# The loads of the heads' queries, keys and values in a memory cross-attention, chained in the order of their use

## Chip, core and metric

The kernel runs on one core of a Trainium2 chip. A core has a matmul engine (PE, with its weight loads shown apart as PEld), a vector engine (DVE), a scalar engine (ACT), a general engine (POOL) and a sync engine (SP), each with its own queue of instructions that it works off in order; a transfer (DMA) is issued from such a queue and then runs beside it. The metric is the device time of one execution in microseconds, lower is better, given as the median of three runs.

## The reference

One layer of an encoder is applied to two groups of tokens, 512 "sample" tokens (S) and 256 "prompt" tokens (P), with a width of 1024, in float32: a gated feed-forward block, a mixer, an attention over a memory of 256 tokens for each group, and a second feed-forward block, each followed by a layer norm. The change lies in the attention:

```
def memory_cross_attention(x, mem, w_q, w_kv, w_o):
    q = (x @ w_q).reshape(B, T, XA_HEADS, XA_HEAD_DIM)          # 4 heads of 256
    k, v = jnp.split(mem @ w_kv, 2, axis=-1)
    ...
    s = jnp.einsum('bthd,bmhd->bhtm', q, k) * (XA_HEAD_DIM ** -0.5)
    p = jax.nn.softmax(s, axis=-1)
    o = jnp.einsum('bhtm,bmhd->bthd', p, v).reshape(B, T, D_MODEL)
    return o @ w_o
```

## The kernel before

Every float32 matrix product is made of three matmuls on operands that are split into a high part and a rest (`split`, L84 on ACT and L85 on DVE; `mm3`, L103 to L105 on PE). A program orders the instructions of each engine ahead of the run; `tc.issue_after(x)` tells it that what is issued inside comes after x.

The attention (function `attention`) has these stages. Keys and values of both memories are made first (`keys_values`, run in pieces between other work, the rest of it by `drain()`, L1194). They don't stay on the chip: each head's keys go to a buffer in device memory (`kd[h]`), its values to `vd[h]`. Then the queries of the four heads are made, one head at a time, by `products` (L472) from sums of the input that lie in the tiles qS1, qS2 and qS4 (each as a high and a low tile, in the pool "sums"); each head's queries go to `qd[h]` by two stores (L1229, issued from ACT). The weights for a head's queries are loaded and combined by `weights_of` (loads L444).

Then the heads are worked off. `scores(h, s)` multiplies queries with keys (tile sc), takes the row maximum (DVE, L1259), the exponentials (ACT, L1264) and divides by the row sums (half on POOL, L1267, half on DVE, L1268). `probs_T(h, s)` transposes the result (tile pT, L1277) and splits it into tile p. `values(h, s)` multiplies it with the values (tile ov) and splits the result into xh and xl. The loop that orders them does, for h = 0, 1, 2: the scores of head h+1 for S, the transposes of head h for S, the scores of head h+1 for P, the transposes of head h for P, the value products of head h for both; the scores of head 0 stand ahead of it, the transposes and value products of head 3 run inside `tok_out`, the product with w_o (tile to). So a head's queries and keys are needed one pass before its values.

`fetch(h, parts)` brings a head's parts back: 12 KB per partition of queries (q), 8 KB of keys (k), 8 KB of values (v), each by one transfer issued from SP (L1213). Queries and keys of even heads go to the pool "even", those of odd heads to the pool "odd", one tile each, so that head 2's take the place of head 0's, and head 3's that of head 1's; values take turns in two tiles of "odd". The pool "odd" is opened once "sums" is closed and takes its memory, so that its first loads wait until PE has read the sums for the last time. SP issues in order: a load that waits holds all that is behind it in SP's queue, among it the weights of w_o (raw, L93), which are told to come after the last fetch (L1321).

Of the kernel before, what the change touches and what calls it, by code (L numbers as in the profile page):

```python
# [7 lines left out]
F32 = mybir.dt.float32  # L8
# [47 lines left out]
def _encoder(ctx, tc, nc, io, out, dbg):  # L56
# [6 lines left out]
    def psum(name):  # L63
        return pp.tile([128, 512], F32, tag="ps", name=name)
# [13 lines left out]
    def nid(p):  # L78
        uid[0] += 1
        return f"{p}{uid[0]}"  # L80
# [21 lines left out]
    def mm3(o, lh, ll, rh, rl, start, stop):  # L102
        nc.tensor.matmul(o, lh, rh, start=start, stop=False)  # L103
        nc.tensor.matmul(o, lh, rl, start=False, stop=False)  # L104
        nc.tensor.matmul(o, ll, rh, start=False, stop=stop)  # L105
# [89 lines left out]
    def fill(ns):  # L195
        while ns > 0 and pending:
            try:
                ns -= next(pending[0])
            except StopIteration:
                pending.pop(0)  # L200

    def drain():
        fill(1e12)
# [878 lines left out]
    def attention():  # L1082
# [9 lines left out]
        def opened(name, side="left"):  # L1092
            stack[name] = ExitStack()
            return stack[name].enter_context(tc.tile_pool(name=name, bufs=1, reuse_waits="tile", side=side))
# [75 lines left out]
        def ring(offs, n):  # L1170
            turn = [0]

            def get():
                turn[0] += 1
                o = offs[turn[0] % len(offs)]
                return flat[:, o:o + n]
            return get
# [4 lines left out]
        _, weights_of, _, products, _ = seven(X, sg, 1, ring([n * 512 for n in range(4)], 512), snap_t, sum_t)  # L1182
# [7 lines left out]
            last_sum = sums(X, (snap_t, sum_t), k, *a)  # L1190
        fill(FILL[2])
        wq = io["w_xq"]
        marks["dve"] = last_sum
        drain()  # L1194
        ws = weights_of(wq[0], wq[1])
        stack["mem"].close()

        ev, od = opened("even", "right"), None
        tl, last_fetch = {}, [None]

        def fetch(h, parts):
            pool = ev if h % 2 == 0 else od
            for p in parts:
                if p == "q":
                    t = pool.tile([128, 2, 2, TT], F32R, tag="q", bufs=1, name=nid("q"))
                    src = qd[h][:]
                elif p == "k":
                    t = pool.tile([128, 2, 2, 512], F32R, tag="k", bufs=1, name=nid("k"))
                    src = kd[h][:]
                else:  # L1210
                    t = od.tile([128, 4, 2, 256], F32R, tag="v", bufs=2, name=nid("v"))
                    src = vd[h][:]
                last_fetch[0] = nc.sync.dma_start(t[:].bitcast(F32), src)  # L1213
                tl[p, h] = t

        fetch(0, "k")
        qs = opened("qs", "right")
        for h in range(4):
            g1, x, u1, u2 = products(ws)
            for b, parts in ((1, (u1, u2)), (0, (g1, x))):  # L1220
                t = qs.tile([128, 2, TT], F32R, tag="qst", bufs=2, name=nid("qst"))
                for n, p in enumerate(parts):
                    hi, lo = [t[:, y, n * HT:(n + 1) * HT] for y in range(2)]
                    nc.scalar.activation(hi, p, AF.Copy, scale=-1.0 if b else 1.0)
                    if b:
                        ins = V.scalar_tensor_tensor(lo, p, -1.0, hi.bitcast(F32), ALU.mult, ALU.subtract)
                    else:
                        ins = V.tensor_tensor(lo, p, hi.bitcast(F32), op=ALU.subtract)
                nc.scalar.dma_start(qd[h][:, b], t[:].bitcast(F32))  # L1229
            marks["dve"] = ins.ins  # L1230
            if h < 3:
                with behind():
                    ws = weights_of(wq[2 * h + 2], wq[2 * h + 3])
            if h == 1:
                fetch(0, "q")
        stack["qs"].close()
        stack["sums"].close()
        od = opened("odd")
        fetch(1, "qk")
        fetch(0, "v")  # L1240

        es, pr = {}, {}

        def scores(h, s):
            q, kk = tl["q", h], tl["k", h]
            m0 = 0 if s is S else 256
            ms = slice(m0, m0 + 256)
            e2 = sg.tile([128, 1024], F32, tag="stg" if s is S else "raw", bufs=2 if s is S else 1, name=nid("e"))
            es[h, s] = e2
            for tp in range(s.nt // 2):  # L1250
                ps = psum(nid("sc"))
                for u in range(2):
                    tcs = slice(s.off + (2 * tp + u) * 128, s.off + (2 * tp + u + 1) * 128)
                    for b in range(2):
                        mm3(ps[:, u * 256:(u + 1) * 256], q[:, b, 0, tcs], q[:, b, 1, tcs],
                            kk[:, b, 0, ms], kk[:, b, 1, ms], b == 0, b == 1)
                mx = sp.tile([128, 2], F32, tag="mx", name=nid("mx"))
                sm = sp.tile([128, 2], F32, tag="sm", name=nid("sm"))
                V.tensor_reduce(mx[:], ps[:].rearrange("p (a b) -> p a b", b=256), AX.X, ALU.max)  # L1259
                V.tensor_scalar(mx[:], mx[:], -1.0 / 16, None, ALU.mult)  # L1260
                e = e2[:, tp * 512:tp * 512 + 512]
                for u in range(2):
                    us = slice(u * 256, (u + 1) * 256)
                    nc.scalar.activation(e[:, us], ps[:, us], AF.Exp, bias=mx[:, u:u + 1], scale=1.0 / 16,  # L1264
                                         accum_out=sm[:, u:u + 1])
                V.reciprocal(sm[:], sm[:])
                nc.gpsimd.tensor_scalar(e[:, 0:256], e[:, 0:256], sm[:, 0:1], None, ALU.mult)  # L1267
                V.tensor_scalar(e[:, 256:512], e[:, 256:512], sm[:, 1:2], None, ALU.mult)  # L1268

        def probs_T(h, s):  # L1270
            p = od.tile([128, 2, 2, s.T], F32R, tag="p" + s.name, bufs=1, name=nid("p"))
            pr[h, s] = p
            for m in range(2):
                ps = psum(nid("pT"))
                for t in range(s.nt):
                    c = t * 256 + m * 128
                    nc.tensor.transpose(ps[:, t * 128:(t + 1) * 128], es[h, s][:, c:c + 128], ident[:])  # L1277
                split(p[:, m, 0, :], p[:, m, 1, :], ps[:, :s.T])

        def values(h, s):  # L1280

            v, p = tl["v", h], pr[h, s]
            m0 = 0 if s is S else 2
            for b in range(2):
                ps = psum(nid("ov"))[:, :s.T]
                c = slice(b * 128, (b + 1) * 128)
                for m in range(2):
                    mm3(ps, v[:, m0 + m, 0, c], v[:, m0 + m, 1, c], p[:, m, 0, :], p[:, m, 1, :], m == 0, m == 1)
                split(xh[s.name][:, 2 * h + b, :], xl[s.name][:, 2 * h + b, :], ps)
# [3 lines left out]
        for h in range(3):  # L1293
            scores(h + 1, S)
            probs_T(h, S)
            scores(h + 1, P)
            if h < 2:
                fetch(h + 2, "qk")
            fetch(h + 1, "v")
            probs_T(h, P)  # L1300
            values(h, S)
            values(h, P)
# [128 lines left out]
    mixer(1)  # L1431
    x3 = dp.tile([128, 6, D], F32, name="x3")
    attention()
    ffn_fast(2, 3, front2, [0, 1, 2, 3, 4, 5], x3, ((9, 10), (1, 2), (3, 4), (5, 6)), [0, 7, 8])
    glob["accp"].close()
# [80 lines left out]
```

## Time and profile before

| | |
|---|---|
| median of 3 runs | 1778.63 us (1777.95 to 1780.29) |
| the profiled execution, its own time | 1777.02 us |
| its span in the profile | 1775.2 us |
| PE busy | 1748.7 us (99% of the span) |
| DVE / ACT / POOL busy | 1266.5 / 753.0 / 38.6 us |
| all DMA | 271.96 MB, 153 GB/s over the span |

The page gives the busy time of each engine over the span; the chain of waits follows the work that ended last back from its end; the timeline lists instructions in order with the idle time ahead of them and what ended it; the table of windows gives busy time, granted PE clock and DMA rate for chosen stretches. All times are microseconds from the start of the span. The scores, transposes and value products lie between 1150 and 1215 us.

### The profile page before, as it was taken

The numbers are of one execution on the slowest core, as the hardware profiler recorded it, in microseconds if no ns is written. First come the engines' busy times: TensorE is split into PE (matmuls) and PEld (weight loads), VectorE is DVE, ScalarE is ACT, GpSimd is POOL, SyncE is SP. The second block draws the span as 40 slices with busy tenths as digits, with TensorE's granted clock in tenths as the row PEclk, the third lists the DMA queues.
The fourth block names the chain that finished last, engine by engine and source line by source line (L and its number), as shares of the span: only waits on it lengthen the run. The fifth ranks groups of instructions, "written<-read, shape, count | busy, mean of one in ns | idle before, by whom it ended". The sixth has DMA issues, their size and how long they took to land.

```text
span 1775.2 us, 24813 instructions
## 1 busy us (share of the span) xinstructions
PE 1748.7 (99%) x9518; PEld 1605.4 (90%) x9518; DVE 1266.5 (71%) x2191; ACT 753.0 (42%) x1303; POOL 38.6 (2%) x72
## 2 busy tenths in 40 slices
PE   9999999999999999999999999979999999999998
PEld 9999999988899999888888888968899999998886
DVE  8777777597668654678775975555887777766966
ACT  6444444453235544645232243442244444444431
POOL 0000000000100000000000000020000000000002
PEclk9999999999999999999999999989999999999999
DMA  5433333687333334211464545475324333327951
GB/s 197 140 121 116 125 125 107 214 312 257 124 112 109 125 125 141 84 48 49 136 207 156 189 143 193 160 311 189 132 74 138 116 125 121 127 98 292 339 179 71
DMA packets 106038, 271.96 MB, mean 153 GB/s; under 512 B 10400, under 2 KB 32672, under 8 KB 104384
## 3 DMA queue, kind: packets, MB, share of 16 engines
q1 hardware_dynamic: 91776, 239.97, 38.9%
q10 hardware_dynamic: 14144, 30.41, 4.5%
q8 instruction: 74, 1.21, 0.3%
q14 instruction: 44, 0.36, 0.1%
HBM read 206.12 MB, written 64.23 MB: 152 GB/s over the span
## 4 chain that ended last, share of the span: by engine, by line
PE 95%; DVE 2%; DMA 2%; ACT 1%; issue 0%; SPq 0%; ACTq 0%; DVEq 0%
PE px L472 24%; PE dn L283 13%; PE py L472 12%; PE pz L472 6%; PE pt L103 5%; PE pt L104 5%; PE pt L105 5%; PE to L103 2%; PE to L105 2%; PE to L104 2%; PE dn L105 2%; PE dn L104 2%; PE dn L103 2%; PE pp L472 1%; PE lt L188 1%; PE V L105 1%
## 5 line engine op out<-in xcount | busy, mean ns | idle before, releaser
L84 ACT ACTIVATE wh<-raw 128x512 fp32r<-128x512 f32 (+2 forms) x281 | 221.0, 789 | 266.6 <-PE pt L104 83.8
L85 DVE TENSOR_TENSOR wl<-raw,wh 128x512 fp32r<-128x512 f32 (+2 forms) x281 | 248.7, 887 | 94.2 <-ACT wh L84 93.9
L283 PE MATMUL dn<-wh,ao 128*128 128x512 f32 x600 | 185.3, 389 | 0.0
L283 PEld LDWEIGHTS dn<-wh,ao 128*128 128x128 f32 x600 | 112.6, 188 | 23.5
L103 PE MATMUL pt<-xh,wh 128*128 128x512 f32 (+2 forms) x384 | 129.9, 338 | 0.0
L104 PE MATMUL pt<-xl,wh 128*128 128x512 f32 (+2 forms) x384 | 129.3, 337 | 0.0
L105 PE MATMUL pt<-xh,wl 128*128 128x512 f32 (+2 forms) x384 | 128.9, 336 | 0.0
L84 ACT ACTIVATE wh<-tt 128x512 fp32r<-128x512 f32 x156 | 94.0, 624 | 72.0 <-PE px L472 60.5
L283 PE MATMUL dn<-wl,ao 128*128 128x512 f32 x300 | 116.7, 389 | 0.0
L85 DVE TENSOR_TENSOR wl<-tt,wh 128x512 fp32r<-128x512 f32 x156 | 104.0, 685 | 3.0 <-ACT wh L84 2.2
L472 PE MATMUL px<-xh,wl 128*128 128x384 f32 x280 | 93.5, 334 | 0.0
L472 PE MATMUL px<-xh,wh 128*128 128x384 f32 x280 | 93.5, 334 | 0.0
L472 PE MATMUL px<-xl,wh 128*128 128x384 f32 x280 | 93.5, 334 | 0.0
L549 DVE SCALAR_TENSOR_TENSOR h<-sil,sum 128x384 f32<-128x384 f32 x78 | 43.5, 557 | 54.8 <-ACT sil L548 54.8
L103 PEld LDWEIGHTS pt<-xh,wh 128*128 128x128 f32 x384 | 72.7, 189 | 7.3 <-issue 0.5
L105 PEld LDWEIGHTS pt<-xh,wl 128*128 128x128 f32 x384 | 72.7, 189 | 6.5
L104 PEld LDWEIGHTS pt<-xl,wh 128*128 128x128 f32 x384 | 72.7, 189 | 6.3 <-issue 0.2
L103 PE MATMUL to<-wh,xh 128*128 128x512 f32 x192 | 75.0, 390 | 0.0
L104 PE MATMUL to<-wl,xh 128*128 128x512 f32 x192 | 74.7, 389 | 0.0
L105 PE MATMUL to<-wh,xl 128*128 128x512 f32 x192 | 74.7, 389 | 0.0
L84 ACT ACTIVATE ao<-sr 128x768 fp32r<-128x768 f32 x50 | 41.9, 844 | 69.8 <-issue 25.0
L548 ACT ACTIVATE sil<-sum 128x384 f32<-128x384 f32 x39 | 20.5, 525 | 111.4 <-DVE sum L484 111.4
(404 smaller groups left out, 4789.4 us busy)
## 6 DMA issues: line engine op xcount, KB each, us to landing
raw<-in_ffn_gu_dram SPq DMA_DIRECT2D x84, 512.0 KB, 3.5
raw<-in_ffn_dn_dram SPq DMA_DIRECT2D x64, 512.0 KB, 5.4
raw<-in_w_mix_dram SPq DMA_DIRECT2D x32, 512.0 KB, 3.5
sr<-sspill SPq DMA_DIRECT2D x32, 384.0 KB, 5.2
sspill<-hs SPq DMA_DIRECT2D x56, 192.0 KB, 1.9
hspill<-hq SPq DMA_DIRECT2D x12, 768.0 KB, 3.7
hr<-hspill SPq DMA_DIRECT2D x24, 384.0 KB, 6.0
x<-acc SPq DMA_DIRECT2D x18, 512.0 KB, 2.6
```

The source lines that it names most:

```text
L84: nc.scalar.activation(hi, src, AF.Copy)
L85: (lo_eng or nc.vector).tensor_tensor(lo, src, hi.bitcast(F32), op=ALU.subtract)
L103: nc.tensor.matmul(o, lh, rh, start=start, stop=False)
L104: nc.tensor.matmul(o, lh, rl, start=False, stop=False)
L105: nc.tensor.matmul(o, ll, rh, start=False, stop=stop)
L188: nc.tensor.transpose(ps[:, j * 128:(j + 1) * 128], A[:, c:c + 128], ident[:])
L283: nc.tensor.matmul(ps[t][:], l, r[:, o], start=start and k == 0 and m == 0, stop=stop and k == 1 and m == 2, skip_group_check=True)
L472: nc.tensor.matmul(ps, l[:, c], r[:, k, :], start=st and n == 0, stop=sp_ and n == 2, skip_group_check=True)
L548: nc.scalar.activation(sil[:], g, AF.Silu)
L549: ins = nc.vector.scalar_tensor_tensor(h32[:, half * HT:(half + 1) * HT], sil[:], -0.5, u, ALU.mult, ALU.mult)
```

## The change

Three edits in `attention`. Each fetch is told to be issued after the one before it (`issue_after` with the last fetch). The keys of a head are fetched ahead of its queries, and in the loop the values of head h+1 ahead of the keys and queries of head h+2. And the first weights of the queries are asked for ahead of `drain()`.

```
-        drain()
         ws = weights_of(wq[0], wq[1])
+        marks["dve"] = last_sum
+        drain()
...
-                last_fetch[0] = nc.sync.dma_start(t[:].bitcast(F32), src)
+                with ExitStack() as order:
+                    if last_fetch[0]:
+                        order.enter_context(tc.issue_after(last_fetch[0].ins))
+                    last_fetch[0] = nc.sync.dma_start(t[:].bitcast(F32), src)
...
-        fetch(1, "qk")
+        fetch(1, "kq")
         fetch(0, "v")
...
+            fetch(h + 1, "v")
             if h < 2:
-                fetch(h + 2, "qk")
-            fetch(h + 1, "v")
+                fetch(h + 2, "kq")
```

On PE and POOL no instruction stands elsewhere than before; the third edit changes only the numbers of tiles. On SP the fetches stand as follows, before. A tile's name is followed by a running number; after the arrow stands the source, whose digit is the head (qd2 holds the queries of head 2). In brackets is what the instruction waits for: PE, or transfers (DMAHW and a slot).

```order
L1213 DMA q1536_10327<-qd0_8743 128x3072 [waits DMAHW6_49,DMAHW5_49,DMAHW4_49]
L1213 DMA q1583_10729<-qd2_8745 128x3072 [waits DMAHW2_49,DMAHW6_49,DMAHW1_49,PE_49]
L1213 DMA q1555_10572<-qd1_8744 128x3072 [waits DMAHW7_49,DMAHW0_49]
L1213 DMA k1556_10574<-kd1_8736 128x2048
L1213 DMA v1557_10576<-vd0_8739 128x2048
L1213 DMA k1584_10731<-kd2_8737 128x2048
L1213 DMA v1585_10733<-vd1_8740 128x2048
L1213 DMA q1607_10865<-qd3_8746 128x3072 [waits DMAHW4_49,DMAHW6_49,DMAHW3_49,PE_49]
L1213 DMA k1608_10867<-kd3_8738 128x2048 [waits DMAHW7_49]
L1213 DMA v1609_10869<-vd2_8741 128x2048 [waits DMAHW5_49,DMAHW0_49,PE_49]
L1213 DMA v1631_11001<-vd3_8742 128x2048 [waits DMAHW2_49,PE_49]
```

The same place on SP with the change:

```order
L1216 DMA q1536_10327<-qd0_8743 128x3072 [waits DMAHW6_49,DMAHW5_49,DMAHW4_49]
L1216 DMA k1555_10572<-kd1_8736 128x2048 [waits DMAHW1_49,PE_49]
L1216 DMA q1556_10574<-qd1_8744 128x3072 [waits DMAHW6_49,DMAHW7_49,DMAHW0_49,PE_49]
L1216 DMA v1557_10576<-vd0_8739 128x2048 [waits PE_49]
L1216 DMA v1583_10729<-vd1_8740 128x2048 [waits DMAHW1_49]
L1216 DMA k1584_10731<-kd2_8737 128x2048 [waits DMAHW1_49,PE_49]
L1216 DMA q1585_10733<-qd2_8745 128x3072 [waits DMAHW2_49]
L1216 DMA v1607_10865<-vd2_8741 128x2048 [waits DMAHW7_49,DMAHW3_49,PE_49]
L1216 DMA k1608_10867<-kd3_8738 128x2048 [waits DMAHW5_49,DMAHW4_49]
L1216 DMA q1609_10869<-qd3_8746 128x3072 [waits DMAHW6_49]
L1216 DMA v1631_11001<-vd3_8742 128x2048 [waits DMAHW0_49,PE_49]
```

The queries of head 2 stood ahead of the keys and queries of head 1 and now stand behind them and behind both first value loads. The values of head 2 stood behind the queries and keys of head 3 and now stand ahead of them.

On ACT, in the pass that makes the scores of head 3 and the values of head 2, before (wh is the high part of a weight of w_o, p1632 the transposed probabilities of head 2 for P, e1627 the exponentials of head 3 for P):

```order
L84 ACTIVATE p1624_10963<-pT1626_10971 128x512
L84 ACTIVATE p1632_11003<-pT1633_11004 128x256
L84 ACTIVATE p1632_11003<-pT1634_11009 128x256
L84 ACTIVATE wh1642_11053<-raw1641_11052 128x1024
L1264 ACTIVATE e1627_10978,sm1630_10993<-sc1628_10979,mx1629_10992 128x256 x2
L84 ACTIVATE xh_3418<-ov1635_11014 128x512
```

and with the change:

```order
L84 ACTIVATE p1624_10963<-pT1626_10971 128x512
L84 ACTIVATE wh1642_11053<-raw1641_11052 128x1024
L84 ACTIVATE p1632_11003<-pT1633_11004 128x256
L84 ACTIVATE p1632_11003<-pT1634_11009 128x256
L1267 ACTIVATE e1627_10978,sm1630_10993<-sc1628_10979,mx1629_10992 128x256 x2
L84 ACTIVATE xh_3418<-ov1635_11014 128x512
```

The first split of a w_o weight moved ahead of the two copies of p for P. (The second such split moved ahead by two copies of xh in the same way, and DVE's parts of both with them.)

On SP, at the parameters of the layer norm behind the attention (ln_g, ln_b), before:

```order
L93 DMA raw1673_11297<-in_w_xo_dram 128x1024
L150 DMA ln_g20_11193<-in_ln_g_dram 128x512
L150 DMA ln_g21_11195<-in_ln_g_dram 128x512
L150 DMA ln_b20_11197<-in_ln_b_dram 128x512
L150 DMA ln_b21_11199<-in_ln_b_dram 128x512
L93 DMA raw1676_11315<-in_w_xo_dram 128x1024
```

and with the change:

```order
L93 DMA raw1673_11297<-in_w_xo_dram 128x1024
L93 DMA raw1676_11315<-in_w_xo_dram 128x1024
L150 DMA ln_g20_11193<-in_ln_g_dram 128x512
L150 DMA ln_g21_11195<-in_ln_g_dram 128x512
L150 DMA ln_b20_11197<-in_ln_b_dram 128x512
L150 DMA ln_b21_11199<-in_ln_b_dram 128x512
```

The last weight of w_o moved ahead of the four parameter loads.

More of the change, by code (lines that the diff above doesn't have):

```diff
@@ L1192, in attention @@
         wq = io["w_xq"]
+        ws = weights_of(wq[0], wq[1])
         marks["dve"] = last_sum
         drain()
-        ws = weights_of(wq[0], wq[1])
         stack["mem"].close()
```

## The prediction

> **What bounds the kernel now.** First the page: PE is busy nearly all the time, so time is lost only where PE idles or runs slowly.
>
> ```profile
> span 1775.2 us, 24813 instructions
> ...
> PE 1748.7 (99%) x9518; PEld 1605.4 (90%) x9518; DVE 1266.5 (71%) x2191; ACT 753.0 (42%) x1303; POOL 38.6 (2%) x72
> ```
>
> 1775.2 − 1748.7 leaves 26.5 us of idle PE. Next the waits of the stretch around the attention (1070 to 1240): who waited, for whom, the sum, how often, the longest.
>
> ```profile
> PE sc L103 <- DMA k<-kd: 12.6, 1, 12.6
> ...
> PE py L472 <- ACT acc L477: 1.9, 1, 1.9
> ```
>
> One wait of PE, for keys, is nearly half of all its idle time. The chain of waits around it (start, length, what):
>
> ```profile
> 1148.21 2.08 PE px L472 x12
> 1154.63 0.33 SPq L1213
> 1155.05 0.38 SPq L1213
> 1155.49 11.59 DMA k<-kd
> 1167.21 0.55 PE sc L103
> ```
>
> The keys of head 1 are issued at 1155.49 as the third load of a row; the two ahead of them are the queries of heads 2 and 1. Why so late, SP's own waits tell:
>
> ```profile
> SPq L1213 <- PE sc L105: 13.4, 1, 13.4
> ```
>
> SP stood 13.4 us at the queries of head 2, which wait until PE is through with the scores of head 0, since they take the place of head 0's queries. Head 1's keys and queries stand behind it in SP's queue. PE's timeline shows the gap and the pass behind it:
>
> ```profile
> 1154.20 0.28 PE L104 MATMUL sc<-k,q 128*128 128x256 f32 x1
> 1154.33 0.28 PE L105 MATMUL sc<-k,q 128*128 128x256 f32 x1
> 1167.21 0.55 PE L103 MATMUL sc<-k,q 128*128 128x256 f32 x1 [12.61 <-DMA k<-kd]
> ...
> 1179.82 0.28 PE L103 MATMUL sc<-k,q 128*128 128x256 f32 x1
> ```
>
> Head 1's scores start at 1167.21, head 2's at 1179.82. Later on the same timeline, a value product of head 1 and the first score of head 3:
>
> ```profile
> 1186.81 0.50 PE L104 MATMUL ov<-p,v 128*128 128x512 f32 x1
> ...
> 1189.96 0.28 PE L103 MATMUL sc<-k,q 128*128 128x256 f32 x1
> ```
>
> The pass from head 2's to head 3's scores has the same matmuls as the one before and takes 1189.96 − 1179.82 = 10.14 us; that one took 1179.82 − 1167.21 = 12.61. The table of windows tells why (PE busy time, then the other engines, PE clock, DMA share, GB/s):
>
> ```profile
> 1080.00:1100.00 20.00, 18.11 (x89) 15.86 (x89) 6.68 (x10) 5.69 (x11) 0.00 (x0) 1.00 0.53 171
> ...
> 1158.00:1160.00 2.00, 0.00 (x0) 0.00 (x0) 0.00 (x0) 0.00 (x0) 0.38 (x1) 0.74 1.03 436
> ...
> 1170.00:1172.00 2.00, 2.00 (x11) 2.00 (x11) 0.86 (x2) 0.87 (x4) 0.00 (x0) 0.50 1.01 426
> 1172.00:1174.00 2.00, 2.00 (x17) 2.00 (x16) 1.29 (x5) 0.97 (x4) 0.44 (x1) 0.84 0.82 336
> ```
>
> The granted clock falls to half during the gap (0.74 in 1158 to 1160, so from about 1158.96, 4.4 us after PE went idle at 1154.33 + 0.28) and is full again at about 1172.6: the first 5 us after the gap ran at half speed. The 1.9 us wait in 1080 to 1100 left the clock at 1.00.
>
> **The change, part by part.** *The gap.* Now keys and queries of head 1 stand ahead of head 2's. They wait for PE's last reading of the sums, of which these matmuls are the last (qS1, qS2, qS4 in turn):
>
> ```profile
> 1139.56 0.33 PE L472 MATMUL py<-qS1h,wl 128*128 128x384 f32 x1
> ...
> 1141.64 0.33 PE L472 MATMUL px<-qS2h,wl 128*128 128x384 f32 x1
> ...
> 1143.72 0.33 PE L472 MATMUL py<-qS4h,wl 128*128 128x384 f32 x1
> ```
>
> By the sizes (6 KB per partition for each of the six tiles of sums, 8 KB of k, then 12 KB of q) k lies over qS1 and q ends within qS2, so k can go at about 1139.9, q at 1142.0, both values by 1144.1. What two such loads take, head 3's show, by SP's timeline and their times to landing (one row of the table of DMA issues for each; the last number is us to landing):
>
> ```profile
> 1157.28 0.49 SPq L1213 DMA_DIRECT2D v<-vd  x1
> 1175.05 0.32 SPq L1213 DMA_DIRECT2D q<-qd  x1
> 1175.42 0.44 SPq L1213 DMA_DIRECT2D k<-kd  x1
> 1180.01 10.46 SPq L1213 DMA_DIRECT2D v<-vd  x2
> ...
> 1207.79 0.90 SPq L150 DMA_DIRECT2D ln_g<-in_ln_g_dram  x2
> ...
> 1212.68 0.33 SPq L93 DMA_DIRECT2D raw<-in_w_xo_dram  x1
> ```
>
> ```profile
> k<-kd SPq DMA_DIRECT2D x1, 1024.0 KB, 8.7
> ```
>
> ```profile
> v<-vd SPq DMA_DIRECT2D x1, 1024.0 KB, 6.9
> ```
>
> ```profile
> v<-vd SPq DMA_DIRECT2D x1, 1024.0 KB, 17.2
> ```
>
> The pair took from 1175.05 to 1175.42 + 8.7 = 1184.1, so 9.1 us. From 1142.0 that is 1151.1, ahead of 1154.45, when PE wants it (1154.33 and another step of about 0.12): the slack of 3.3 us is the cover, and beyond it every microsecond late is one of PE. So the gap of 1167.21 − 1154.45 = **12.76 us** goes, and with it the half clock, 12.61 − 10.14 = **2.47 us**: together 15.23.
>
> [...]
>
> *What is late next: the softmax of head 0.* It had the gap to finish in. On DVE, the last division of head 0 and, in the pass from head 2's scores on, the first row maximum:
>
> ```profile
> 1156.88 0.35 DVE L1268 TENSOR_SCALAR e<-e,sm 128x256 f32<-128x256 f32 x1
> ...
> 1181.45 0.69 DVE L1259 TENSOR_REDUCE mx<-sc 128x2 f32<-128x512 f32 x1 [0.59 <-PE sc L105]
> ...
> 1182.89 0.69 DVE L1259 TENSOR_REDUCE mx<-sc 128x2 f32<-128x512 f32 x1 [0.55 <-PE sc L105]
> ...
> 1196.88 0.75 DVE L85 TENSOR_TENSOR p<-pT,p 128x256 fp32r<-128x256 f32 x2
> ```
>
> In that pass the product at 1186.81 waits for a split at the end of a chain over DVE and ACT that begins with the maximum at 1181.45: 5.36 us. In head 1's pass, begun at 1154.45 instead, that chain can't begin before DVE is through with head 0, at 1156.88 + 0.35 = 1157.23, so the product comes at 1162.59. PE would be there 1186.81 − 1179.82 = 6.99 us after 1154.45, at 1161.44. The price is **1.15 us**; at best 0.6, since DVE idles 0.55 within the chain, ahead of its second maximum, waiting for PE, which can now close up. So head 2's scores start at 1154.45 + 10.14 + 1.15 = 1165.74, which is 14.08 us earlier than 1179.82. Head 2's keys and queries are issued when head 0's scores end, at about 1154.7, nothing of size ahead of them; with the pair's 9.1 us they are there at 1163.8, and cost nothing.
>
> *The wait that is moved: head 2's values ahead of head 3's keys and queries.* That load waits until PE is through with the values of head 0, which is where head 2's scores begin; it was issued at 1180.01, 0.19 after them, and held nothing but the last value load and what follows that. Now it comes at 1165.93, and the keys and queries of head 3 are queued behind it in SP, with head 3's scores waiting for them on PE at 1165.74 + 10.14 = 1175.88. Before, the same three loads took from 1175.05 to 1180.01 + 6.9 = 1186.9, so 11.9 us (the third came late, though the transfers were still at work). The row of six loads, twice the bytes, ran from 1154.7 to 1157.28 + 17.2 = 1174.5, so 19.8 us; half of that is 9.9. Between them I take 11.5, nearer to the row of the same three: landing at 1177.4, a wait of **1.6 us**, with 0 (at 9.9) and 2.0 (at 11.9) as the bounds. Like the 1.9 us above it should leave the clock alone.
>
> [...]
>
> *The w_o weights.* The first split on ACT now stands ahead of the copies of p for P. On ACT before, and the first product on PE that needs those copies:
>
> ```profile
> 1194.94 1.34 ACT L84 ACTIVATE p<-pT 128x512 fp32r<-128x512 f32 x3
> 1196.18 1.06 ACT L84 ACTIVATE wh<-raw 128x1024 fp32r<-128x1024 f32 x1
> ```
>
> ```profile
> 1198.68 0.28 PE L103 MATMUL ov<-p,v 128*128 128x256 f32 x1
> ```
>
> The copies end 1.06 later, at 1197.34, and DVE's 0.75 behind them at 1198.1, ahead of 1198.68: hidden by 0.6 us. If the weight has not landed, ACT stands there and every microsecond beyond 0.6 is PE's. It is issued behind the last value load, which waits for the values of head 1 alone and so doesn't take part in the 1.6 us; seen from head 3's scores it comes 1.6 earlier, and ACT asks 0.8 to 1.3 earlier. I take nothing, with 0 to 1.0 as the bounds.
>
> *The layer norm's parameters* are issued at 1207.79 before and would wait, behind the last weight, until 1212.68. They are first used here:
>
> ```profile
> 1239.89 0.74 DVE L169 SCALAR_TENSOR_TENSOR acc<-acc,mv,ln_g 128x512 f32<-128x512 f32 x1
> ```
>
> 27 us of cover: nothing. The third edit moves no instruction on any engine, only tiles' numbers: nothing. The matmuls, and what follows the attention, are the same.
>
> *Sum.* 12.76 + 2.47 − 1.15 − 1.6 = 12.48 us less, at the bounds 15.23 − 0.6 = 14.6 and 15.23 − 1.15 − 2.0 − 1.0 = 11.1. The profiled execution took 1777.02 us by its own time (span 1775.2), 1.6 below the median of 1778.63; its counterpart would be 1764.5, its span 1762.7. Against the median: 1778.63 − 12.48 = **1766.1**, bounds 1764.0 and 1767.5.
>
> **Rivals.** *No new wait.* Softmax and three loads are both absorbed: 1778.63 − 15.23 = 1763.4. Against it: the DVE chain is bound by rows, not by a guess on transfers. 0.10.
>
> *Head 3's wait grows past the clock's patience.* If the three loads land 4.4 us late, the clock halves again and the pass behind it pays another 2.47: 14.08 − 4.4 − 2.47 = 7.2 gained, 1771.4; just short of the halving 1768.9. For it: DMA stands at over 0.9 of its share in such a row of loads. Against: it needs 14.3 us where 11.9 was the most seen. 0.08.
>
> *The change doesn't do what it says.* If the wait of head 1's keys for PE were one for the scores of head 0 and not for the sums, they would go at 1154.7 and the pair land at 1163.8; PE would still wait 9.5 us at half clock, gain 1167.2 − 1163.9 = 3.3, and lose the 1.6 at head 3: 1776.9. Against it: their tile takes the place of the sums, and the values now stand with a wait for PE of their own. 0.03.
>
> *The half clock costs half of its whole length.* If PE's idle time at half clock counted too, 6.84 us would go instead of 2.47: 12.76 + 6.84 − 1.15 − 1.6 = 16.85, so 1761.8. [...] Against it stand the two passes, which differ by 2.47 only. 0.02.
>
> *Slower.* The same place as the 1.6 us: head 3's keys and queries, held in SP behind head 2's values. The gain up to there is 14.08; with the half clock of 2.47 a wait of 11.6 eats it, which means landing 1187.5, 21.6 us after the first of the three is issued. Up to then it is a gain, beyond it a loss: at 27 us, 17.0 of wait, 1784. For it: a queue that holds three loads behind one wait for PE is what cost 12.6 us before. Against it: twice the bytes took 19.8. 0.02.
>
> **How the numbers follow.** The forecast's case, both waits within their bounds, has 0.72; 0.03 are for what I have not named. The runs before lie from 0.7 below to 1.7 above their median. The range takes the forecast's case and that of no new wait, with 0.7 below it: 1762.7; above, the wait of head 3 up to where the clock halves, 1768.9, and 1.6 for the runs: 1770.5. Some 3.6 us, 0.2%, is what a measurement can tell from no change: faster by more are the forecast, no new wait, the grown wait, the idle half clock and 0.02 of the unnamed, 0.94; within it, the change that does nothing and the other 0.01, 0.04; slower, 0.02.
>
> **What would show it.** Right: head 1's keys and queries are issued at about 1140 and 1142 and landed by 1151; PE's scores run through from head 0 to head 1; the clock stays at 1.00 between 1150 and 1200; PE waits about 1 us at head 0's value products for DVE's split of p, and 1 to 2 us at head 3's scores for the queries; head 2's scores start near 1165.7 and the product with w_o 12.5 us earlier than before. Wrong: a wait of several microseconds at head 1's scores (the loads don't go early), a clock of 0.5 anywhere in the attention (head 3's loads), a wait of PE for p at head 2 with ACT idle ahead of a w_o split (the weights), or a loss of like size in a stage that the change doesn't touch.

## The result, and the profile after

| | before | after |
|---|---|---|
| median | 1778.29 us (4 runs, 1777.95 to 1780.29) | 1765.6 us (4 runs, 1765.14 to 1765.65 without the one named below) |
| profiled execution: own time, span | 1777.02, 1775.2 | 1765.55, 1763.8 |

The ratio after to before is 0.9924, with a 95% interval of 0.9908 to 0.9941: 12.7 us less, where 12.48 were forecast, and 1765.6 beside 1766.1. One of the four runs of after, at 2123 us with a mean clock of 0.76, was disturbed and is left out of the ratio. That the sum came out so close hides two things that the traces show: a cost of about 1 us that the prediction did not have, and a spread between executions that is larger.

The page of the profile after, its span and the engines' totals:

```profile
span 1763.8 us, 24812 instructions
...
PE 1747.5 (99%) x9518; PEld 1604.1 (91%) x9518; DVE 1266.7 (72%) x2191; ACT 752.6 (43%) x1303; POOL 38.4 (2%) x72
```

PE's idle time fell from 26.5 to 1763.8 − 1747.5 = 16.3 us, and its busy time by 1.2. (Matmuls overlap in the records, 0.28 us each at a step of 0.12 in the scores, so busy time shows the half clock only partly: 1.2 us here, where the passes of before differ by 2.47.) SP's timeline of after, the loads in the order of their issue:

```profile
1139.82 0.33 SPq L1216 DMA_DIRECT2D k<-kd  x1
1141.89 0.32 SPq L1216 DMA_DIRECT2D q<-qd  x1
1143.97 1.28 SPq L1216 DMA_DIRECT2D v<-vd  x2
1154.53 0.32 SPq L1216 DMA_DIRECT2D k<-kd  x1
...
1166.83 0.32 SPq L1216 DMA_DIRECT2D v<-vd  x1
...
1167.67 0.43 SPq L1216 DMA_DIRECT2D q<-qd  x1
```

Head 1's keys go at 1139.82 and its queries at 1141.89, both first values at 1144; head 2's keys at 1154.53; and head 2's values at 1166.83 now stand ahead of head 3's queries at 1167.67. PE's timeline of after, at the same places as before:

```profile
1154.22 0.28 PE L105 MATMUL sc<-k,q 128*128 128x256 f32 x1
1154.34 0.28 PE L103 MATMUL sc<-k,q 128*128 128x256 f32 x1
...
1160.72 0.50 PE L103 MATMUL ov<-p,v 128*128 128x512 f32 x1 [0.53 <-ACT p L84]
...
1163.49 0.50 PE L104 MATMUL ov<-p,v 128*128 128x512 f32 x1 [0.63 <-DVE p L85]
...
1166.64 0.28 PE L103 MATMUL sc<-k,q 128*128 128x256 f32 x1
...
1178.46 0.36 PE L103 MATMUL sc<-k,q 128*128 128x256 f32 x1 [1.53 <-DMA q<-qd]
...
1202.38 0.40 PE L103 MATMUL to<-wh,xh 128*128 128x512 f32 x1
```

The last matmul of head 0's scores (1154.22) and the first of head 1's (1154.34) follow each other at the usual step of 0.12: the 12.61 us wait is gone. The waits that are left are 0.53, 0.23 (not in these rows) and 0.63 us at head 0's value products and 1.53 at head 3's scores. The last row is the first product with w_o behind the last value products; before it stood here, by PE's timeline:

```profile
1213.80 0.40 PE L103 MATMUL to<-wh,xh 128*128 128x512 f32 x1
```

From the last matmul of head 0's scores to this product, before took 1213.80 − 1154.33 = 59.47 us and after 1202.38 − 1154.22 = 48.16. These **11.31 us** are what the attention gained; I call this stretch the attention from here on. The table of windows of after (PE busy, the other engines, PE clock, DMA share, GB/s):

```profile
1150.00:1160.00 10.00, 10.00 (x86) 9.85 (x84) 6.33 (x19) 4.57 (x17) 3.54 (x4) 1.00 1.01 405
1160.00:1170.00 10.00, 8.61 (x55) 7.00 (x54) 6.86 (x17) 6.13 (x19) 2.59 (x3) 1.00 0.61 232
1170.00:1180.00 10.00, 8.41 (x59) 7.38 (x57) 6.54 (x18) 5.74 (x18) 3.26 (x3) 1.00 0.92 366
```

The clock stays at 1.00, and the transfers now run full (1.01) in 1150 to 1160, beside the last products of the queries' projection and the first scores. That is where the unforeseen cost arises. The chain of waits of after, from the last store of the queries to head 3's scores:

```profile
1151.34 8.63 DMA qd<-qst
1160.14 0.43 issue
1160.57 1.02 ACT e L1267 x4
...
1163.49 0.50 PE ov L104
...
1167.67 10.66 DMA q<-qd
1178.46 0.36 PE sc L103
```

It now runs through a store, the last block of head 3's queries on its way from the staging tile qst to device memory. By the groups of DMA issues in 1136 to 1190, such a store (the last number is the median in us to landing) took before

```profile
qd<-qst ACTq DMA_DIRECT2D x3, 768.0 KB, 3.3
```

and after

```profile
qd<-qst ACTq DMA_DIRECT2D x3, 768.0 KB, 8.6
```

The stores are issued by ACT when they always were (1151.34 here, 1151.44 before), but the loads that SP now issues early run beside them. ACT's first copy of p, by the order, waits for two of these stores, since its tile takes the memory of qst. On ACT's timeline of after:

```profile
1160.07 0.60 ACT L84 ACTIVATE p<-pT 128x512 fp32r<-128x512 f32 x1 [1.02 <-PE pT L1280]
...
1184.43 1.06 ACT L84 ACTIVATE wh<-raw 128x1024 fp32r<-128x1024 f32 x1 [0.33 <-DMA raw<-in_w_xo_dram]
```

The view puts the 1.02 us ahead of 1160.07 down to PE's transposition. But the transpositions that this copy reads were done by 1158.32 on PE's timeline, and the store issued at 1151.34 landed at 1159.97; in e4 and e9 below the view names the store itself. (The second row is the split of the first w_o weight that now stands ahead of the copies of p: ACT waited 0.33 us for the weight, PE nothing.)

### The profile page after: what moved, and what is told of

Read it like the earlier page. It is cut to its first block, busy times and chain, and to the rows that moved or that the text cites. A ratio compares the mean times of both kernels' runs of the same rounds, so it can differ in the third digit from the quotient of the medians.

```text
span 1763.8 us, 24812 instructions
## 1 busy us (share of the span) xinstructions
PE 1747.5 (99%) x9518; PEld 1604.1 (91%) x9518; DVE 1266.7 (72%) x2191; ACT 752.6 (43%) x1303; POOL 38.4 (2%) x72
## 4 chain that ended last, share of the span: by engine, by line
PE 97%; DMA 2%; DVE 1%; ACT 0%; issue 0%; ACTq 0%; POOL 0%; DVEq 0%; SPq 0%; POOLq 0%
PE px L472 25%; PE dn L283 13%; PE py L472 12%; PE pz L472 6%; PE pt L103 5%; PE pt L104 5%; PE pt L105 5%; PE pp L472 3%; PE to L103 2%; PE to L105 2%; PE to L104 2%; PE dn L104 2%; PE dn L105 2%; PE dn L103 2%; PE lt L188 1%; PE V L105 1%
```

## How small differences are read here

The change was timed twice: 1765.6 and 1767.76 us. In seven of the eleven profiles below (e1, e2, e3, e5, e8, e9, e11), the last matmul of head 0's scores lies 1.6 to 1.9 us later than in after's first profile, though PE has the same work up to there. The clock makes the difference. Near 1098 every profile has a wait of PE for ACT, of 1.70 to 2.11 us, that no edit touches. In these seven the clock stands at 0.50 for 3.41 us behind it; in the other six, before and after among them, it stays at 1.00. PE's timeline and the windows (PE clock is the third number from the end), first of after, then of e1:

```profile
1097.91 0.44 PE L472 MATMUL py<-qS4h,wh 128*128 128x384 f32 x1 [2.02 <-ACT acc L477]
```

```profile
1097.13:1100.54 3.41, 2.63 (x15) 2.63 (x16) 1.55 (x3) 2.62 (x6) 0.00 (x0) 1.00 0.44 146
```

```profile
1097.95 0.62 PE L472 MATMUL py<-qS4h,wh 128*128 128x384 f32 x1 [2.04 <-ACT acc L477]
```

```profile
1098.05:1101.46 3.41, 3.41 (x11) 3.41 (x12) 0.88 (x2) 1.89 (x4) 0.00 (x0) 0.50 0.45 154
```

The executions without a trace seem to differ in the same way. Before's runs beside the experiments took 1776.42 to 1777.99 us at a mean clock of 0.995 (14 runs) and 1777.92 to 1780.27 at 0.993 or 0.994 (18 runs), and 3.41 us at half clock lower the mean over such a span by 0.001. Medians therefore don't tell effects of 1 or 2 us apart, and I read such effects from the length of the attention as defined above, which begins behind that place. Three profiles of the same order of instructions (after, e11, e8) gave 48.16, 47.79 and 47.53 us there: a spread of 0.6.

| run | what differs from after | median us (runs) | ratio to before, 95% | attention us |
|---|---|---|---|---|
| before | | 1778.2 | | 59.47 |
| after | | 1765.6 (4) | 0.9908 to 0.9941 | 48.16 |
| e11 | nothing | 1767.76 (5) | 0.9932 to 0.9956 | 47.79 |
| e8 | third edit undone | 1765.97 (4) | 0.992 to 0.9949 | 47.53 |
| e1 | chain alone, old order | 1763.62 (5) | 0.9909 to 0.9934 | 45.53 |
| e12 | e1 again | 1763.66 (4) | 0.9906 to 0.9933 | 45.55 |
| e2 | order alone, no chain | 1775.64 (10) | 0.9979 to 0.9998 | 56.96 |
| e3 | head 1's values late | 1769.54 (5) | 0.9942 to 0.9967 | 51.48 |
| e10 | e3, w_o's splits held back | 1764.57 (5) | 0.9915 to 0.9942 | 47.07 |
| e4 | head 2's values late | 1765.15 (5) | 0.9915 to 0.9942 | 46.72 |
| e5 | both values late | 1764.85 (5) | 0.9915 to 0.994 | 45.55 |
| e7 | both first values ahead of head 1's pair | 1767.64 (4) | 0.9931 to 0.9964 | 50.07 |
| e9 | 1 MB more of loads beside the stores | 1771.77 (5) | 0.9954 to 0.998 | 52.0 |

## Experiments: which part of the change does it

The change has two parts that bear on the loads: the chain, which keeps them in the order of the code, and the new order of the code. Each was run without the other. The chain alone (e1):

```
-        fetch(1, "kq")
+        fetch(1, "qk")
...
-            fetch(h + 1, "v")
             if h < 2:
-                fetch(h + 2, "kq")
+                fetch(h + 2, "qk")
+            fetch(h + 1, "v")
```

> Only the chain is kept: each fetch after the one before, but queries ahead of keys and, in the loop, head h+2's queries and keys ahead of head h+1's values, as before the change. Theory (the gain comes from head 1's pair no longer standing behind head 2's queries; two new costs come from the order edits: the first value load of head 1 goes early and slows the last two stores of the queries, for which ACT's first copy of p waits, 1.0 us; and head 2's values stand ahead of head 3's pair, 1.5 us): no gap at head 1's scores, both new waits gone, 1765.6 - 1.0 - 1.5 = about 1763.1. Rival (the order edits are part of the gain): slower than the changed kernel, above 1766.

The order alone (e2):

```
-                with ExitStack() as order:
-                    if last_fetch[0]:
-                        order.enter_context(tc.issue_after(last_fetch[0].ins))
-                    last_fetch[0] = nc.sync.dma_start(t[:].bitcast(F32), src)
+                last_fetch[0] = nc.sync.dma_start(t[:].bitcast(F32), src)
```

> The order edits and the third edit without the chain. The program that orders the instructions then puts head 2's keys ahead of head 1's keys and queries in SP's queue. Theory (what cost 12.6 us was one load that waits for the scores of head 0 ahead of head 1's pair in SP's queue): the gap at head 1's scores is back, about 11 us (three loads land from about 1154.6 on instead of before's three of a larger size), with the half clock behind it: about 1777, within 0.2% of before. Rival (the gain came from keys ahead of queries and values early): no gap, 1766.

Without the chain the gap is back, by the PE timeline of e2:

```profile
1167.50 0.56 PE L103 MATMUL sc<-k,q 128*128 128x256 f32 x1 [11.09 <-DMA q<-qd]
```

SP again holds a load of head 2 (its keys, issued at 1156.44, when PE is through with head 0's scores) ahead of head 1's, PE waits 11.09 us and the clock falls to 0.50. The order of the code alone is worth 2.5 us in the trace (1775.64 in the runs). The chain alone brings all of the gain and more: 1763.62, and 45.53 us in the attention, 2.6 less than the change. In PE's timeline of e1, from the first scores to the product with w_o, this is the only wait left that the view names, and ACT's first copy of p has none:

```profile
1163.97 0.50 PE L104 MATMUL ov<-p,v 128*128 128x512 f32 x1 [0.63 <-DVE p L85]
```

```profile
1160.56 0.60 ACT L84 ACTIVATE p<-pT 128x512 fp32r<-128x512 f32 x1
```

So the new order costs two waits that the old one doesn't have: that for the stores and that at head 3's scores. Chain alone and change were then run side by side, with no edit but e1's:

> The chain alone once more, as e1. If the two waits that the order edits bring cost what the trace shows (1.0 us for the stores, 1.5 at head 3's scores), it stays 2 to 2.6 us under the change on the same chip, with 45.5 us in the attention: about 1763. If e1's lead came from the execution alone, the two agree within 1 us.

> The change once more, beside the chain alone on the same chip: 1765.6 by the first runs, and 48.2 us (0.6 either way) from the last matmul of head 0's scores to the last group of w_o.

The chain alone took 1763.24 to 1763.75 us (4 runs), the change 1765.22 to 1771.54 (5 runs): the lead is real. Of the 4.1 us between the medians the attention's 47.79 − 45.55 = 2.24 are explained; 1.3 lay ahead of it in the profiled executions, in the same instructions (e11's has the half clock near 1098, e12's has not), and the run of 1771.54 has no trace. **The chain with the old order beats both kernels.**

## Experiments: the two waits of the new order

Each early value load was put back to its late place alone, and both together. Head 1's values behind head 2's pair (e3):

```
+            if h == 0:
+                fetch(2, "kq")
             fetch(h + 1, "v")
-            if h < 2:
-                fetch(h + 2, "kq")
+            if h == 1:
+                fetch(3, "kq")
```

> As changed, but head 1's values are fetched behind head 2's keys and queries. Theory: only three loads run beside the last two stores of the queries, which land in 4 to 6 us instead of 9; ACT's first copy of p starts about 1.0 us earlier after the first score of head 1; head 3's wait stays at 1.5: 1764.6. Rival (ACT's wait of 1.0 us ahead of the copy of p has nothing to do with the stores but is a late transpose): the wait stays, 1765.6.

Head 2's values behind head 3's pair (e4):

```
+            if h == 1:
+                fetch(3, "kq")
             fetch(h + 1, "v")
-            if h < 2:
-                fetch(h + 2, "kq")
+            if h == 0:
+                fetch(2, "kq")
```

> As changed, but head 3's keys and queries are fetched ahead of head 2's values. Theory: PE's wait of 1.5 us at head 3's scores goes, ACT's wait for the stores stays at about 1.0: 1764.1. Rival (the transfers are the limit, not their order, and head 2's pair or head 3's lands late by as much as before): a wait of over 1 us at head 2's or head 3's scores, 1765 or more.

Both (e5):

```
-            fetch(h + 1, "v")
             if h < 2:
                 fetch(h + 2, "kq")
+            fetch(h + 1, "v")
```

> As changed (chain, keys ahead of queries), but both value loads in the loop behind the next pair. Theory: both new waits go, only the softmax chain on DVE and ACT of 1.15 us is left: 1765.6 - 1.0 - 1.5 = 1763.1, the same as with the chain alone. Rival (what is taken off one place comes back at the next, since the transfers of the attention are the limit): 1765 or more.

In e4 the wait at head 3's scores is gone, and the attention shortens by 48.16 − 46.72 = 1.4. The other wait stays, and here ACT's timeline names the store itself:

```profile
1160.45 0.60 ACT L84 ACTIVATE p<-pT 128x512 fp32r<-128x512 f32 x1 [1.34 <-DMA qd<-qst]
```

In e5 both are gone: 45.55 us, e1's length to 0.02. By their medians alone, 1765.15 and 1764.85, e4 and e5 would speak for their rivals, but the waits that the rivals name are not in the traces, and e5's profile is one of those with the half clock near 1098. In e3 the stores took 5.9 and 4.2 us, ACT's first copy of p had no idle time ahead of it, and head 3's wait stayed at 1.36, as the two theories of these waits want it. Yet e3 came out at 1769.54 instead of faster, with 51.48 us. ACT's timeline of e3, and PE's, show a third wait:

```profile
1185.17 1.06 ACT L84 ACTIVATE wh<-raw 128x1024 fp32r<-128x1024 f32 x1 [2.33 <-DMA raw<-in_w_xo_dram]
```

```profile
1187.67 1.34 PE L103 MATMUL ov<-p,v 128*128 128x512 f32 x3 [2.72 <-ACT p L84]
```

The edit moved the first split of a w_o weight further ahead on ACT, before exponentials and copies of p that PE needs; the weight, behind the last value load in SP's queue, landed 2.33 us too late; PE waited 2.72 and the clock fell behind it, by e3's table of windows (PE clock is the third number from the end):

```profile
1184.00:1188.00 4.00, 1.28 (x10) 1.01 (x9) 1.74 (x3) 2.83 (x8) 0.56 (x2) 1.00 1.02 404
1188.00:1191.00 3.00, 2.95 (x8) 1.84 (x7) 3.00 (x8) 2.62 (x8) 0.66 (x1) 0.52 0.88 274
```

Whether the place of that split was all of it, e10 tells: e3 with the splits of w_o held behind the copies of p of head 2, which leaves the heads' loads and the first three weights of w_o where e3 has them (on SP, one transfer of the residual input, acc, moves ahead of the fourth).

```
-            split(h[:, a:b], l[:, a:b], raw[:, a:b], lo_eng)
+            with ExitStack() as order:
+                if "p" in marks:
+                    order.enter_context(tc.issue_after(marks["p"]))
+                split(h[:, a:b], l[:, a:b], raw[:, a:b], lo_eng)
...
-                split(p[:, m, 0, :], p[:, m, 1, :], ps[:, :s.T])
+                a = split(p[:, m, 0, :], p[:, m, 1, :], ps[:, :s.T])
+                if h == 2 and s is P:
+                    marks["p"] = a.ins
```

> Head 1's values late as in e3, and the splits of w_o held on ACT and DVE behind the copies of p of head 2. If e3's new wait came from the place of the first split on ACT alone, ACT no longer stands idle ahead of the exponentials of head 3 (2.33 us in e3), PE's 2.72 us at head 2's products goes and with it the half clock behind it: from the last matmul of head 0's scores to the last group of w_o 51.5 us falls to about 47.2 (the change's 48.2 without its 1.0 for the stores), the median to about 1764.6. If the weight's late landing itself costs (PE waits for it at its first product), or the clock fell for another reason, it stays within 1 us of e3's 51.5 and 1769.5.

ACT's timeline of e10 has the copies of p ahead of the split, and neither waits:

```profile
1182.04 1.34 ACT L84 ACTIVATE p<-pT 128x512 fp32r<-128x512 f32 x3
1183.26 1.06 ACT L84 ACTIVATE wh<-raw 128x1024 fp32r<-128x1024 f32 x1
```

The attention takes 47.07 us where 47.2 were expected, 4.4 less than e3's, and the median is 1764.57: the place of one split on ACT (with its rest on DVE) cost 4.4 us. It is the wait that the prediction named as the weights' risk; the change itself escapes it with 0.33 us on ACT.

## Experiments: the stores, the values' place and the third edit

If the loads slow the stores, more load must slow them more. e9 sends another copy of 1 MB, from device memory to device memory, into SP's queue behind head 0's values; nothing reads it.

```
         fetch(0, "v")
+        spare = dp.tile([128, 4, 2, 256], F32, name="spare")
+        with tc.issue_after(last_fetch[0].ins):
+            last_fetch[0] = nc.sync.dma_start(spare[:], vd[0][:])
```

> As changed, with one more transfer of 1 MB issued from SP behind head 0's values: a copy of them within device memory that nobody reads. Theory (the last stores of the queries share the transfer engines with the early loads, and ACT's first copy of p waits for them): the stores land about 2.5 us later still, ACT's wait grows from 1.0 to 2 to 3.5 us, head 2's scores come that much later: 1767 to 1768.5. Rival (the wait is not for the stores): ACT's wait stays at 1.0, 1765.6.

The last two stores took 10.5 and 11.3 us, and ACT, then PE, waited for them; ACT's and PE's timelines of e9:

```profile
1164.44 0.60 ACT L84 ACTIVATE p<-pT 128x512 fp32r<-128x512 f32 x1 [3.69 <-DMA qd<-qst]
```

```profile
1165.09 0.79 PE L103 MATMUL ov<-p,v 128*128 128x512 f32 x1 [3.21 <-ACT p L84]
```

The attention grew by 52.0 − 48.16 = 3.84, more than expected: ACT's wait went past 3.5 us, and PE's of 3.21 already took the clock down, by the windows of e9 (a quarter of a microsecond at each edge):

```profile
1163.75:1164.00 0.25, 0.00 (x0) 0.00 (x0) 0.00 (x0) 0.00 (x0) 0.00 (x0) 0.74 1.57 623
1164.00:1165.00 1.00, 0.00 (x0) 0.00 (x0) 0.00 (x0) 0.56 (x2) 0.00 (x0) 0.50 1.01 414
1170.50:1170.75 0.25, 0.25 (x2) 0.17 (x1) 0.00 (x0) 0.00 (x0) 0.01 (x1) 0.61 0.00 0
```

The clock fell at 1163.87 (0.74 is half of the quarter at 0.50) and was back at 1170.70: 6.83 us. With e1, e3, e5, e10 and e12 (1 MB less early: stores of 4.2 to 7.4 us, no wait), after, e4, e8 and e11 (8.1 to 9.2 us, waits of 0.45 to 1.34) and e9 (10.5 to 11.3, 3.69), the store's time and ACT's wait rise with the loads beside them. Giving p's tiles memory of their own, which would take away the dependence itself, was not tried.

e7 asks what the order within the early loads is worth: both first values ahead of head 1's keys and queries.

```
-        fetch(1, "kq")
         fetch(0, "v")
+        fetch(1, "v")
+        fetch(1, "kq")
...
-            fetch(h + 1, "v")
+            if h > 0:
+                fetch(h + 1, "v")
```

> As changed, but both first value loads stand ahead of head 1's keys and queries, so that these land last of the four. Nothing else in the order of heads 2 and 3 is changed. Theory (cover of about 3 us for head 1's pair, beyond it each microsecond is one of PE): the queries land at about 1159, as the last of the four did, PE stands about 4.6 us at head 1's scores; the softmax chain and the stores hide in that gap (2.2 us back): 1768.0 with a clock at full, up to 1770.4 if the clock falls to half. Rival (the loads have much more cover than that): no gap, 1765.6.

Head 1's queries, now the last of four loads, took 13.3 us to landing; PE's timeline of e7, and its windows:

```profile
1156.77 0.48 PE L103 MATMUL sc<-k,q 128*128 128x256 f32 x1 [2.86 <-DMA q<-qd]
```

```profile
1156.75:1157.00 0.25, 0.23 (x1) 0.23 (x2) 0.00 (x0) 0.00 (x0) 0.25 (x2) 0.81 0.97 410
1157.00:1160.25 3.25, 3.25 (x16) 3.25 (x16) 0.61 (x1) 0.00 (x0) 0.70 (x1) 0.50 1.04 434
1160.25:1160.50 0.25, 0.25 (x3) 0.25 (x3) 0.22 (x2) 0.00 (x0) 0.00 (x0) 0.86 1.62 688
```

A wait of 2.86 us, where 4.6 were expected: the queries landed at 1156.72 and not at 1159. The clock fell as PE resumed, at 1156.90, for 3.42 us; head 1's first scores, up to the transposes behind them, took 4.47 us instead of 2.86. Both are partly given back, since softmax and stores have that time to finish: 50.07 us, 1.9 more than the change.

e8 undoes the third edit, which by the order moves no instruction:

```
-        ws = weights_of(wq[0], wq[1])
         marks["dve"] = last_sum
         drain()
+        ws = weights_of(wq[0], wq[1])
```

> As changed, with the third edit undone (the weights of the queries asked for behind the drain). No instruction changes its place, so every theory expects the changed kernel's time: 1765.6, within 0.5.

1765.97 us and 47.53 us in the attention: within the spread of the change's own profiles.

## Why the prediction was right, and where it was not

**The gap, 12.76: right.** The keys were issued at 1139.82 and the queries at 1141.89 (forecast 1140 and 1142), the pair had landed by 1150.2 (1151), and PE went from head 0's to head 1's scores without a wait. e2 shows that it is the chain that does this.

**The half clock, 2.47: right.** The clock stays at 1.00. The rival that a half clock costs half of its whole length would have made the attention 4.4 us shorter than the forecast; it came out longer. e7 is the case where half of the length holds: PE worked through the slow stretch of 3.42 us, half of which is an estimate of 1.7 us, and the scores lost 4.47 − 2.86 = 1.61.

**The softmax of head 0, 1.15: right in itself.** In e1, where nothing else waits, head 2's scores begin 11.29 us after the last of head 0's; without the step of 0.12 and the plain pass of 10.14 that leaves 1.03. The product that waits for the split begins 1163.97 − 1155.84 = 8.13 us after the last of head 0's scores, where 1162.59 − 1154.33 = 8.26 were forecast. No run takes this chain away, so its share rests on the timelines.

**The step that failed: the wait at head 0's value products, put down to the softmax chain alone.** The prediction has the product wait "for a split at the end of a chain over DVE and ACT" and for nothing else. In after head 2's scores begin 1166.64 − 1154.22 = 12.42 us after the last of head 0's instead of 11.41: a term of 1.0 us was missing. Against e1's 11.29, the stores cost 1.13 us in after, 0.58 in e11 (11.87) and 1.45 in e4 (12.74). The prediction asked what the early loads need and whether they arrive; it did not ask what they run beside. The stores of the last queries, 3.3 us before, took 8.6, and the memory of their tile is what p needs next. Head 2's queries, issued at 1154.89 while the last of these stores was on its way, landed at 1165.7 instead of 1163.8, which used up their cover: they cost nothing in after, and 0.39 us in e8. That the stores are issued by ACT and the loads by SP did not keep them apart: 3.3 against 8.6 us.

**Head 3's wait, 1.6: right.** It was 1.53 in after and 1.68 in e11, though 0.80 in e8; the last of the three loads landed 11.5 us after the first was issued (1178.33 − 1166.83), the value taken. e4 takes it away with the order that the prediction made responsible.

**w_o's split, the parameters and the third edit, 0:** no wait of PE shows for the first two, and e8 shows none for the third. But the bound of 1.0 on the split was too low as a risk: e3 shows 4.4 when the weight is 2.3 us late, since the clock goes too.

**The sum: close by luck.** With the measured terms it is 12.76 + 2.47 − 1.03 − 1.13 − 1.53 = 11.54; the attention gained 11.31, and 11.68 and 11.94 in the other two profiles of this order. For the profiled execution the prediction named 1764.5, with a span of 1762.7. It took 1765.55, with 1763.8: there the missing 1.0 us shows. In the median's 12.7 it does not, and the second batch gave 10.3, since a median moves by as much with the number of executions that have the half clock near 1098. (The first runs of before have no clock on record, so that this is what hid the 1.0 us is likely and not shown.)

**The clock's patience, 4.4 us, behind the rival of head 3's wait: wrong.** It was read from one long gap of before. e3, e7 and e9 lost the clock with PE waits of 2.72, 2.86 and 3.21 us, and the wait near 1098 cost it in e9 with 1.95 and left it alone in e4 with 2.09. Head 3's 1.53 in after and 1.68 in e11 left it alone. So that rival could decide far below its 4.4 us, and the forecast 1.6 stood close to e9's 1.95. The 1.9 us wait of before, on which the prediction relied for the clock, was no safe sign: it is the wait near 1098 that costs the clock in seven other profiles.

## What to carry to other kernels

When a load is moved forward, ask not only what it waits for and who waits for it, but which transfers it will now run beside, stores issued by other engines included (here they took 8.6 us instead of 3.3), and whose memory those hold. When a chain cures a queue that stands behind one wait, try it with the old order first: here the chain was the whole gain, and reordering the code beside it gave back 2.0 to 2.6 us. And where an order is decided by a scheduler, look at what an edit of the loads does to the other engines' order: one weight's split that moved on ACT cost 4.4 us. Before you explain a difference of 1 to 2 us between medians, look at the granted clock ahead of the stage that you changed: here a wait of 2 us that no edit touched made seven of 13 profiles later by 1.6 to 1.9.

## What the runs showed of the hardware

Measured by windows of a quarter of a microsecond, as for e7 and e9 above, the stretches at half clock in the attention lasted 3.41 us in e3, 3.42 in e7, 6.83 in e9, 10.24 in e2 and 13.65 in before, which is one, one, two, three and four times 3.41; behind the wait near 1098 it was 3.41 too.

The time from PE's last work to the fall of the clock was not the same from case to case. In before PE had been idle for 4.4 us (from 1154.61 to 1158.97), in e2 for 3.9 (from 1156.41 to 1160.35), in e9 for 2.0 (from its last transposition's end at 1161.88 to 1163.87). In e3 and e7 PE was at work again, 0.5 and 0.1 us behind its waits of 2.72 and 2.86, when the clock fell (at 1188.14 and 1156.90). Nor did the length of a wait of about 2 us decide: near 1098 the clock fell behind 1.95 us in e9, where PE's matmuls then follow each other at 0.32 us instead of 0.17, and not behind 2.09 in e4, where the step stays at 0.17 to 0.19. What decides there, these runs do not show. Such a wait lost the clock in seven of 13 profiles, which are 1.6 to 1.9 us later for it; in e7 the half clock cost 1.61.

The last two stores of the queries, 768 KB each and issued by ACT, took 3.3 us with no loads beside them (before, e2), 4.2 to 7.4 beside 3.5 MB of early loads (e1, e3, e5, e10, e12), 8.1 to 9.7 beside 4.5 MB (after, e4, e7, e8, e11) and 10.5 to 11.3 beside 1 MB more (e9).
